# Output product: two pairs of output tiles computed together with the input features outermost, and the merge's first tile moved from GpSimd to VectorE

## The chip, the cores and the metric

One core of a Trainium2 chip runs the whole program. The metric is the device time of one execution in microseconds, from the first to the last instruction with what lies around them; the number given for a kernel is the median of its runs. The engines are named as in the profile: PE is TensorE's matrix products, PEld its weight loads, DVE is VectorE, ACT is ScalarE, POOL is GpSimd, SP issues the transfers.

## The reference

Two layers over 256 positions of 1024 features. Each layer normalises, feeds three token mixers (retention, forgetting attention, RWKV-7) from one combined projection, merges the three branches by gates, multiplies by `w_out` and adds to the residual; then comes a SwiGLU feed-forward block with its own norm. Cut to the part around the change:

```python
gates = sigmoid(gate_c).reshape(B, S, 3, D)
merged = (gates[:, :, 0] * (y_ret @ p_ret[l])
          + gates[:, :, 1] * (y_fox @ p_fox[l])
          + gates[:, :, 2] * (y_rwkv @ p_rwkv[l]))
x = x + merged @ w_out[l]
h = rmsnorm(x, ffn_norm[l])
gu = h @ w_gate_up[l]
g, u = split(gu, 2, axis=-1)
x = x + (silu(g) * u) @ w_down[l]
```

## The kernel before

Activations are held features by positions: 1024 features are eight tiles of 128 partitions by 256 positions, handled as four pairs (128 x 512). A product keeps fp32 accuracy by splitting both operands in a rounded part and the rest (`hi` and `lo`, for weights `whi` and `wlo`), and adds three matmuls for each 128 x 128 weight block: hi by whi (line L290), then the two mixed ones (L293 and L294). Function `mm3` issues them; with `late` set, the matmul that needs the activation's `lo` is the last of the three instead of the second.

Weights arrive from HBM in 1 MB transfers of 16 blocks (`raw`, three buffers) and are split in pieces of 8 blocks: ACT writes `whi` (L273, 128 x 1024) and DVE then writes `wlo` as the difference (L274). There are four buffers of each. A piece can be overwritten only when PE has done its last matmul with it.

The stage of interest is the end of the mixers. For the third branch (`bb == 2`, RWKV) a loop over the four pairs `c` computes 12 matmuls with `p_rwkv` into PSUM; DVE multiplies the result by the gate (L567, scalar_tensor_tensor, one operand in PSUM); an addition merges it in place with the sum of the other two branches (L569); and `split` turns the merged pair in `hi` (ACT, L376) and `lo` (L377). For `c == 0` the addition and the `lo` are on POOL, for the other three on DVE.

The output product follows at once in `layer`. Pair `j` of its outputs needs all eight merged tiles as inputs. For `j == 0` `gemm_halves(mx, 4)` takes 16 blocks: both output tiles over input tiles 0 to 3, then both over 4 to 7, `late`. Pairs 1 and 2 go one output tile after the other (`gemm_pair`), pair 3 by `gemm_halves` without a cut. DVE adds the residual (L491), and ACT and DVE make the norm's operands (L392, L393, L403, L406, L407).

The code is written as generators with paces. A scheduling layer turns it into a fixed list of instructions for each engine when the program is built; the priorities `hp_merge` (44) and `hp_turn` (0) act there: what stands in `early("hp_merge")`, the multiplication and the addition, is taken 44 steps earlier than its place in the code, the split is not. On the chip each engine goes through its own list.

Of the kernel before, what the change touches and what calls it, by code (L numbers as in the profile page):

```python
# [8 lines left out]
F32 = mybir.dt.float32  # L9
# [4 lines left out]
ALU = mybir.AluOpType  # L14
AX = mybir.AxisListType

P = 128
T = 256
DM = 1024
KT = DM // P  # L20
# [71 lines left out]
def pack_inputs(inp, depth=DEPTH):  # L92
    f = {k: np.asarray(v) for k, v in inp.items()}
    out = {}

    def fm(a, n):
        return a.reshape(n, P).T

    out["xt"] = np.ascontiguousarray(f["x"][0].T.reshape(KT, P, T).transpose(1, 0, 2))
    out["const"] = np.concatenate([CONSTS[k] for k in C_ORDER], 1)  # L100
    pr = []
    for l in range(depth):
        fb = np.broadcast_to(f["fox_f_bias"][l][None, :], (P, 4))
        cols = {
            "mixg": fm(f["mix_norm"][l], 8), "ffng": fm(f["ffn_norm"][l], 8), "mu": fm(f["rwkv_mu"][l], 8),
            "w0": fm(f["rwkv_w0"][l], 2), "a0": fm(f["rwkv_a0"][l], 2), "kk": fm(f["rwkv_k_k"][l], 2),
            "ka": fm(f["rwkv_k_a"][l], 2), "rk": fm(f["rwkv_r_k"][l], 2), "rgn": fm(f["rwkv_gn"][l], 2),
            "retgn": fm(f["ret_gn"][l], 2),
            "fq": np.tile(f["fox_q_norm"][l], 2)[:, None], "fk": np.tile(f["fox_k_norm"][l], 2)[:, None],
            "fb": fb, "w2a2": np.concatenate([f["rwkv_w2"][l], f["rwkv_a2"][l]], 0), "g2": f["rwkv_g2"][l],  # L110
        }
        pr.append(np.concatenate([cols[k] for k, _ in PARAMS], 1))
    out["par"] = np.ascontiguousarray(np.stack(pr))

    def tiles(w, cols, nk):
        return w[:, cols].reshape(nk, P, -1, P).transpose(1, 2, 0, 3)

    R, F, W, G = 0, 1024, 1024 + 772, 1024 + 772 + 1024
    order = np.concatenate([
        np.arange(W, W + 1024),  # L120
        np.arange(R, R + 512), np.arange(R + 768, R + 1024)])
    win, wqk, wv, wgt = [], [], [], []
    for l in range(depth):
        w = f["w_in"][l]
        t = tiles(w, order, KT)
        win.append(t.reshape(P, N_IN, 2, KT, P).transpose(1, 0, 2, 3, 4).reshape(N_IN, P, 2 * KT * P))
        wqk.append(w[:, F:F + 512].reshape(KT, P, 512).transpose(1, 0, 2).reshape(P, KT * 512))
        vf = w[:, F + 512:F + 772].reshape(KT, P, 260).transpose(1, 0, 2).reshape(P, KT * 260)
        vr = w[:, R + 512:R + 768].reshape(KT, P, 256).transpose(1, 0, 2).reshape(P, KT * 256)
        wv.append(np.concatenate([vf, vr], 1))  # L130
        wgt.append(tiles(w, np.arange(G, G + 3 * DM), KT).reshape(P, 3, 4, 2 * KT * P).transpose(1, 2, 0, 3))
    out["wqk"] = np.ascontiguousarray(np.stack(wqk))
    out["win"] = np.ascontiguousarray(np.stack(win))
    out["wgate"] = np.ascontiguousarray(np.stack(wgt))
    out["wv"] = np.ascontiguousarray(np.stack(wv))
    pp, wo, wg, wd = [], [], [], []
    for l in range(depth):
        pp.append(np.stack([tiles(f[n][l], np.arange(DM), 2).reshape(P, 2 * DM) for n in ("p_ret", "p_fox", "p_rwkv")]))
        wo.append(tiles(f["w_out"][l], np.arange(DM), KT).reshape(P, 4, 2 * KT * P).transpose(1, 0, 2))
        gu = tiles(f["w_gate_up"][l], np.arange(2 * DFF), KT).reshape(P, 2, FT // 2, 2 * KT * P)  # L140
        wg.append(gu.transpose(2, 1, 0, 3))
        wd.append(tiles(f["w_down"][l], np.arange(DM), FT).transpose(1, 0, 2, 3).reshape(4, 2, P, FT, P)
                  .transpose(0, 2, 1, 3, 4).reshape(4, P, 2 * FT * P))
    out["pp"] = np.ascontiguousarray(np.stack(pp))
    out["wo"] = np.ascontiguousarray(np.stack(wo))
    out["wg"] = np.ascontiguousarray(np.stack(wg))
    out["wd"] = np.ascontiguousarray(np.stack(wd))
    return out


class Kernel:
# [156 lines left out]
    def gemm_halves(self, xs, kcut=None, hook=None, tag="mm"):  # L308
# [19 lines left out]
                hook()  # L328
        return ps

    @staticmethod
    def run(gen):
        while True:
            try:
                next(gen)
            except StopIteration as e:
                return e.value
# [125 lines left out]
    def layer(self, l):  # L463
        tc, nc, d = self.tc, self.nc, self.d
        if l == 0:
            self.norm_start(0, "mixg")
            for j in range(4):
                self.norm_add(j, False)
                if j != 2:
                    self.piece()  # L470
        xs = self.xs
        with ExitStack() as st:
            e = st.enter_context
            self.big = e(tc.tile_pool(name="big", bufs=1))
            self.pad(self.big, 24)
            self.t2 = e(tc.tile_pool(name="t2", bufs=13))
            self.sm = e(tc.tile_pool(name="sm", bufs=1))
            self.mixers(l, xs)
            mx = self.mx

            self.norm_start(l, "ffng")
            for j in range(4):
                if j == 0:
                    ps = self.gemm_halves(mx, 4)
                elif j == 3:
                    ps = self.gemm_halves(mx)
                else:
                    ps = self.run(self.gemm_pair(mx))
                x = self.xp.tile([P, 2, T], F32, tag="x", bufs=5, name=self.nm("x"))
                for o, p in self.parts(ps):  # L490
                    nc.vector.scalar_tensor_tensor(out=x[:, o, :], in0=p, scalar=0.5, in1=self.xt[j][:, o, :], op0=ALU.mult, op1=ALU.add)  # L491
                self.xt[j] = x
                self.norm_add(j)
        self.ffn(l)
# [34 lines left out]
    def gemms(self, l, xs, rstd, rn):  # L529
        nc, d = self.nc, self.d  # L530
        fx = []
        self.need = None
        for _ in self.fox_in(l, xs, rn, fx):
            yield PACE["gemms0"]
        self.start.append(("fox", self.fox(l, fx)))
        rt = []
        for _ in self.ret_in(l, xs, rstd, rn, rt):
            yield PACE["gemms1"]
        self.start.append(("ret", self.ret(l, rt)))
        yield PACE["gemms2"]  # L540
        gates = {}
        for b in (0, 1, 2):
            for c in range(4):
                gen = self.gemm_pair(xs)
                while True:
                    try:
                        next(gen)
                    except StopIteration as e:
                        ps = e.value
                        break  # L550
                    yield PACE["gemms3"]
                g = gates[b, c] = self.big.tile([P, 2, T], F32, tag="gate", bufs=8, name=self.nm("gate"))
                nc.vector.tensor_tensor(out=g, in0=ps, in1=self.b2(rstd), op=ALU.mult)  # L553
                nc.scalar.activation(g, g, AF.Tanh, scale=0.5)
                yield PACE["gemms3"]
            if b == 0:
                continue
            for bb in ((0, 1) if b == 1 else (2,)):
                self.need = ("ret", "fox", "rwkv")[bb]
                yield PACE["gemms4"]  # L560
                self.need = None
                y = [(self.y[bb][0][:, k, :], self.y[bb][1][:, k, :]) for k in range(2)]
                for c in range(4):
                    ps = self.run(self.gemm_pair(y))
                    g, m = gates[bb, c], gates[0, c]
                    with self.early("hp_merge"):
                        nc.vector.scalar_tensor_tensor(out=g, in0=g, scalar=1.0, in1=ps, op0=ALU.add, op1=ALU.mult)  # L567
                        if bb:
                            (nc.vector if bb == 2 and c >= 1 else nc.gpsimd).tensor_tensor(out=m, in0=m, in1=g, op=ALU.add)  # L569
                    if bb == 2:  # L570
                        with self.early("hp_turn"):
                            hi, lo = self.split(self.t2, m, [P, 2, T], ("t2", "t2"), nc.gpsimd if c < 1 else nc.vector)
                        self.mx.extend((hi[:, i, :], lo[:, i, :]) for i in range(2))
                    elif c % 2:
                        yield PACE["gemms5"]
# [621 lines left out]
```

## Time and profile before

| | us |
|---|---|
| median of 3 runs | 800.09 (799.79 to 800.15) |
| the profiled execution, its own time | 800.76 |
| its span, first to last instruction | 799.0 |
| PE busy | 783.6 |
| DVE busy | 576.2 |
| ACT busy | 397.1 |
| POOL busy | 61.6 |

The span is that of one execution under the profiler; its own time lies 0.67 us above the median. Busy times of a PE matmul are modelled and overlap, so PE is read by its idle gaps and by the distance from one start to the next. The granted clock of PE is 1.00 in the whole span.

### The profile page before, as it was taken

The page shows a single profiled execution, that of the slowest core. Times are in us where ns is not written, and L with a number is a line of the kernel's source. Part 1 is how long each engine was busy: PE and PEld are TensorE (multiplying, and loading weights), DVE is VectorE, ACT ScalarE, POOL GpSimd, SP SyncE. Part 2 cuts the span into 40 slices and gives each one's busy share as a digit, 9 for nine tenths or more (in the row PEclk, how much of TensorE's full clock was granted, in tenths as well). Part 3 has the DMA queues.
Part 4 walks back from the last instruction along what each step waited for, and adds up shares of the span by engine and source line. Part 5 has one row for each costly group of instructions (what it writes and reads, how often), then busy time and mean ns, then how long its engine had stood idle before and what let it go on. Part 6 is the DMA issues. An engine that isn't in the chain of part 4 may idle for free.

```text
span 799.0 us, 16543 instructions
## 1 busy us (share of the span) xinstructions
PE 783.6 (98%) x7018; PEld 762.5 (95%) x7018; DVE 576.2 (72%) x900; ACT 397.1 (50%) x543; POOL 61.6 (8%) x83
## 2 busy tenths in 40 slices
PE   8999899999999999999999999999999999999998
PEld 6999899999999999999998988999999999999997
DVE  5897979597867666656678798877878666666453
ACT  6367445535645444445444764554456545444331
POOL 3201210031000000000023030101110000000000
PEclk9999999999999999999999999999999999999999
DMA  8565524335454554556554553452445454555650
GB/s 308 208 226 167 170 80 169 140 114 205 161 208 167 203 205 172 191 184 211 200 188 175 197 172 106 162 174 106 142 176 190 180 201 174 206 202 164 211 190 27
DMA packets 27802, 140.42 MB, mean 176 GB/s; under 512 B 7600, under 2 KB 9168, under 8 KB 12496
## 3 DMA queue, kind: packets, MB, share of 16 engines
q1 hardware_dynamic: 27728, 139.36, 50.2%
q8 instruction: 55, 0.90, 0.5%
q14 instruction: 19, 0.16, 0.1%
HBM read 136.97 MB, written 1.33 MB: 173 GB/s over the span
## 4 chain that ended last, share of the span: by engine, by line
PE 88%; DVE 6%; DMA 2%; ACT 1%; issue 1%; POOL 1%; SPq 0%; POOLq 0%; DVEq 0%; ACTq 0%
PE mm L290 26%; PE mm L294 25%; PE mm L293 25%; DVE wlo L274 2%; PE mqk L439 1%; PE mqk L438 1%; PE mqk L437 1%; ACT whi L273 1%; DMA rsw<-rqk 1%; PE pgm L762 1%; DVE rkk L745 1%; DMA raw<-in_win 1%; DMA raw<-in_pp 1%; PE mv L437 1%; PE mv L439 1%
## 5 line engine op out<-in xcount | busy, mean ns | idle before, releaser
L273 ACT CAST whi<-raw 128x1024 fp32r<-128x1024 f32 (+1 forms) x257 | 264.7, 1033 | 321.7 <-PE mm L293 232.2
L274 DVE TENSOR_TENSOR wlo<-raw,whi 128x1024 fp32r<-128x1024 f32 (+1 forms) x257 | 313.3, 1221 | 143.0 <-ACT whi L273 142.3
L290 PE MATMUL mm<-xh,whi 128*128 128x256 f32 x1312 | 368.0, 280 | 0.5 <-ACT whi L273 0.5
L294 PE MATMUL mm<-xh,wlo 128*128 128x256 f32 x1248 | 346.3, 277 | 0.7 <-DVE wlo L274 0.7
L293 PE MATMUL mm<-xl,whi 128*128 128x256 f32 x1248 | 346.3, 278 | 0.0
L290 PEld LDWEIGHTS mm<-xh,whi 128*128 128x128 f32 x1312 | 246.6, 188 | 2.8 <-issue 0.9
L294 PEld LDWEIGHTS mm<-xh,wlo 128*128 128x128 f32 x1248 | 234.4, 188 | 1.1 <-DVE wlo L274 0.9
L293 PEld LDWEIGHTS mm<-xl,whi 128*128 128x128 f32 x1248 | 234.5, 188 | 0.8 <-issue 0.5
L290 PE MATMUL mm<-hi,whi 128*128 128x256 f32 x576 | 160.1, 279 | 0.0
L294 PE MATMUL mm<-hi,wlo 128*128 128x256 f32 x544 | 150.9, 277 | 0.0
L293 PE MATMUL mm<-lo,whi 128*128 128x256 f32 x544 | 150.8, 277 | 0.0
L290 PEld LDWEIGHTS mm<-hi,whi 128*128 128x128 f32 x576 | 108.2, 188 | 0.6 <-issue 0.3
L294 PEld LDWEIGHTS mm<-hi,wlo 128*128 128x128 f32 x544 | 102.1, 188 | 0.2
L293 PEld LDWEIGHTS mm<-lo,whi 128*128 128x128 f32 x544 | 102.1, 188 | 0.1
L569 POOL TENSOR_TENSOR gate<-gate,gate 128x512 f32<-128x512 f32 x10 | 13.3, 1336 | 142.3 <-DVE gate L567 142.3
L600 DVE TENSOR_TENSOR h<-t,mm 128x512 f32<-128x512 f32 x22 | 15.1, 687 | 11.5 <-PE mm L294 8.6
L567 DVE SCALAR_TENSOR_TENSOR gate<-gate,mm 128x512 f32<-128x512 f32 x24 | 16.1, 682 | 8.6 <-PE mm L294 8.5
L597 DVE TENSOR_TENSOR t<-mm,rstd 128x512 f32<-128x512 f32 (+1 forms) x24 | 15.2, 645 | 8.5 <-PE mm L294 8.5
L553 DVE TENSOR_TENSOR gate<-mm,rstd 128x512 f32<-128x512 f32 x24 | 16.5, 689 | 3.8 <-PE mm L294 3.5
L293 PE MATMUL mm<-xh,wlo 128*128 128x256 f32 x64 | 18.0, 281 | 0.7 <-DVE wlo L274 0.7
L439 PE MATMUL mv<-whi,xl 128*128 128x260 f32 (+1 forms) x64 | 18.6, 290 | 0.0
L437 PE MATMUL mv<-whi,xh 128*128 128x260 f32 (+1 forms) x64 | 18.6, 290 | 0.0
(259 smaller groups left out, 797.9 us busy)
## 6 DMA issues: line engine op xcount, KB each, us to landing
raw<-in_wg SPq DMA_DIRECT2D x44, 1024.0 KB, 4.7
raw<-in_wgate SPq DMA_DIRECT2D x24, 1024.0 KB, 4.8
raw<-in_wd SPq DMA_DIRECT2D x16, 1024.0 KB, 5.0
raw<-in_win SPq DMA_DIRECT2D x13, 1024.0 KB, 8.0
raw<-in_wo SPq DMA_DIRECT2D x8, 1024.0 KB, 4.8
raw<-in_pp SPq DMA_DIRECT2D x6, 1024.0 KB
raw<-in_wd SPq DMA_DIRECT2D x8, 768.0 KB, 4.3
raw<-in_wqk SPq DMA_DIRECT2D x4, 1024.0 KB, 5.0
```

The source lines that it names most:

```text
L273: nc.scalar.copy(hi[:, :m * width], r)
L274: nc.vector.tensor_tensor(out=lo[:, :m * width], in0=r, in1=hi[:, :m * width].bitcast(F32), op=ALU.subtract)
L290: nc.tensor.matmul(out, wh, xh, start=first, stop=False)
L293: nc.tensor.matmul(out, wh, xl, start=False, stop=False)
L294: nc.tensor.matmul(out, wl, xh, start=False, stop=last)
L437: nc.tensor.matmul(out, xh[:, s], wh, start=first, stop=False)
L439: nc.tensor.matmul(out, xl[:, s], wh, start=False, stop=last)
L553: nc.vector.tensor_tensor(out=g, in0=ps, in1=self.b2(rstd), op=ALU.mult)
L567: nc.vector.scalar_tensor_tensor(out=g, in0=g, scalar=1.0, in1=ps, op0=ALU.add, op1=ALU.mult)
L569: (nc.vector if bb == 2 and c >= 1 else nc.gpsimd).tensor_tensor(out=m, in0=m, in1=g, op=ALU.add)
L597: nc.vector.tensor_tensor(out=t[:, o, :], in0=p, in1=self.bs(rstd, o), op=ALU.mult)
L600: nc.vector.tensor_tensor(out=h, in0=t, in1=pu, op=ALU.mult)
```

## The change

Four edits.

1. `w_out` is packed anew on the host: of the first 16 output-by-input groups, the blocks of one pair of input tiles for four output tiles now make a piece of 8, so that one piece serves pairs 0 and 1 for that pair of input tiles. The transfers keep their size and number.
2. A new `gemm_quad` computes output pairs 0 and 1 together, with the pair of input tiles (`kk`) outermost: 24 matmuls for merged pair 0, then 24 for pair 1, and so on. Each output pair accumulates in one PSUM tile. Its `mm3` isn't `late`.
3. `layer` calls it once; the two results are taken over by the residual addition one after the other, each as one 128 x 512 instruction.
4. In the merge of the third branch the addition is on POOL only for `c == 1`, and every `lo` is on DVE.

```diff
-        wo.append(tiles(f["w_out"][l], np.arange(DM), KT).reshape(P, 4, 2 * KT * P).transpose(1, 0, 2))
+        t = tiles(f["w_out"][l], np.arange(DM), KT)
+        head = t[:, :4].reshape(P, 4, 4, 2 * P).transpose(2, 0, 1, 3).reshape(2, 2, P, 8 * P).transpose(0, 2, 1, 3)
+        wo.append(np.concatenate([head.reshape(2, P, 16 * P), t[:, 4:].reshape(P, 2, 16 * P).transpose(1, 0, 2)]))
...
+    def gemm_quad(self, xs):
+
+        ps = [self.ps.tile([P, 2, T], F32, tag="mm", bufs=4, name=self.nm("mm")) for _ in range(2)]
+        for kk in range(KT // 2):
+            for j in range(2):
+                for m in range(2):
+                    for k in range(2 * kk, 2 * kk + 2):
+                        if not self.cur:
+                            self.refill()
+
+                        self.mm3(ps[j][:, m, :], self.block(), xs[k], k == m == 0, k == KT - 1 and m == 1)
+        return ps
...
                 if j == 0:
-                    ps = self.gemm_halves(mx, 4)
-                elif j == 3:
-                    ps = self.gemm_halves(mx)
-                else:
-                    ps = self.run(self.gemm_pair(mx))
+                    both = self.gemm_quad(mx)
+                ps = both[j] if j < 2 else self.run(self.gemm_pair(mx)) if j == 2 else self.gemm_halves(mx)
...
-                            (nc.vector if bb == 2 and c >= 1 else nc.gpsimd).tensor_tensor(out=m, in0=m, in1=g, op=ALU.add)
+                            (nc.vector if bb == 2 and c != 1 else nc.gpsimd).tensor_tensor(out=m, in0=m, in1=g, op=ALU.add)
                     if bb == 2:
                         with self.early("hp_turn"):
-                            hi, lo = self.split(self.t2, m, [P, 2, T], ("t2", "t2"), nc.gpsimd if c < 1 else nc.vector)
+                            hi, lo = self.split(self.t2, m, [P, 2, T], ("t2", "t2"))
```

The instruction lists differ only between the third branch's merge and the first residual additions, in both layers alike (lines of the changed kernel are 3 to 16 higher). Shown is the first layer. Names: `mm_2467`, `mm_2490`, `mm_2509` and `mm_2534` are the third branch's products for pairs 0 to 3; `gate_1200`, `gate_1319`, `gate_1443` and `gate_1505` the merged pairs 0 to 3; `hi_2486`/`lo_2487`, `hi_2505`/`lo_2506`, `hi_2530`/`lo_2531`, `hi_2549`/`lo_2550` their splits; `whi_2436`/`wlo_2437` and the next numbers are pieces of `w_out`; `mm_2554` and `mm_2555` are outputs of the output product.

DVE before, from the first multiplication of the third branch to the last split; `lo_2487` isn't in it, since POOL makes it:

```order
L567 SCALAR_TENSOR_TENSOR gate_2243<-gate_2243,mm_2467 128x512
L567 SCALAR_TENSOR_TENSOR gate_2327<-gate_2327,mm_2490 128x512
L569 TENSOR_TENSOR gate_1319<-gate_1319,gate_2327 128x512
L274 TENSOR_TENSOR wlo_2513<-raw_2510,whi_2512 128x1024
L567 SCALAR_TENSOR_TENSOR gate_2402<-gate_2402,mm_2509 128x512
L567 SCALAR_TENSOR_TENSOR gate_2464<-gate_2464,mm_2534 128x512
L569 TENSOR_TENSOR gate_1443<-gate_1443,gate_2402 128x512
L569 TENSOR_TENSOR gate_1505<-gate_1505,gate_2464 128x512
L377 TENSOR_TENSOR lo_2506<-gate_1319,hi_2505 128x512
```

DVE after, the same stretch:

```order
L580 SCALAR_TENSOR_TENSOR gate_2243<-gate_2243,mm_2467 128x512
L582 TENSOR_TENSOR gate_1200<-gate_1200,gate_2243 128x512
L580 SCALAR_TENSOR_TENSOR gate_2327<-gate_2327,mm_2490 128x512
L277 TENSOR_TENSOR wlo_2513<-raw_2510,whi_2512 128x1024
L580 SCALAR_TENSOR_TENSOR gate_2402<-gate_2402,mm_2509 128x512
L580 SCALAR_TENSOR_TENSOR gate_2464<-gate_2464,mm_2534 128x512
L582 TENSOR_TENSOR gate_1443<-gate_1443,gate_2402 128x512
L582 TENSOR_TENSOR gate_1505<-gate_1505,gate_2464 128x512
L393 TENSOR_TENSOR lo_2487<-gate_1200,hi_2486 128x512
L277 TENSOR_TENSOR wlo_2557<-raw_2510,whi_2556 128x1024
L393 TENSOR_TENSOR lo_2506<-gate_1319,hi_2505 128x512
```

The addition for pair 0 has come in behind its multiplication, that for pair 1 has left, and `lo_2487` stands ninth, behind the multiplications and additions of pairs 2 and 3, where `lo_2506` stood before; `lo_2506` is two places later, behind one more weight split.

PE before, the end of the third branch's products and the start of the output product:

```order
L294 MATMUL mm_2534<-hi_2339,wlo_2407 128x256
L290 MATMUL mm_2554<-hi_2486,whi_2436 128x256
L293 MATMUL mm_2554<-hi_2486,wlo_2437 128x256
L294 MATMUL mm_2554<-lo_2487,whi_2436 128x256
L290 MATMUL mm_2554<-hi_2486,whi_2436 128x256
```

PE after, the same place:

```order
L297 MATMUL mm_2534<-hi_2339,wlo_2407 128x256
L293 MATMUL mm_2554<-hi_2486,whi_2436 128x256
L293 MATMUL mm_2555<-hi_2486,whi_2436 128x256
L296 MATMUL mm_2554<-lo_2487,whi_2436 128x256
L297 MATMUL mm_2554<-hi_2486,wlo_2437 128x256
```

In both, two matmuls stand ahead of the first that reads `lo_2487`. Behind it, before, matmuls of pairs 0 and 1 and of a second output pair alternate; after, 22 matmuls in a row (the one shown among them) need merged pair 0 alone, and then come the 24 of pair 1.

## The prediction

> **What bounds the kernel now.** I read the page's busy times first, then the waits of PE, then the timeline of PE, DVE, POOL and ACT around the longest wait, last the busy times by stretch.
>
> ```profile
> PE 783.6 (98%) x7018; PEld 762.5 (95%) x7018; DVE 576.2 (72%) x900; ACT 397.1 (50%) x543; POOL 61.6 (8%) x83
> ```
>
> PE runs through 98% of the span. Work on another engine therefore counts only where PE waits for it, and a change that leaves the number of matmuls alone can gain at most these waits:
>
> ```profile
> PE mm L294 <- POOL lo L377: 3.1, 2, 1.6
> PE pb L748 <- DVE rkk L745: 2.9, 2, 1.5
> ```
>
> The first row is the place of this change: two waits, one in each layer, for the `lo` of merged pair 0, made by POOL. The second and all smaller ones lie outside the lists that the change touches. On PE's own rows the wait looks like this (start, duration; layer 1, then the same in layer 2):
>
> ```profile
> 197.52 0.28 PE L294 MATMUL mm<-hi,wlo 128*128 128x256 f32 x1
> 197.63 0.28 PE L290 MATMUL mm<-hi,whi 128*128 128x256 f32 x1
> 197.74 0.28 PE L293 MATMUL mm<-hi,wlo 128*128 128x256 f32 x1
> 199.57 0.39 PE L294 MATMUL mm<-lo,whi 128*128 128x256 f32 x1 [1.55 <-POOL lo L377]
> 199.80 0.28 PE L290 MATMUL mm<-hi,whi 128*128 128x256 f32 x1
> ...
> 589.98 0.28 PE L293 MATMUL mm<-hi,wlo 128*128 128x256 f32 x1
> 591.79 0.39 PE L294 MATMUL mm<-lo,whi 128*128 128x256 f32 x1 [1.53 <-POOL lo L377]
> ```
>
> Matmuls start 0.11 us apart; the third one of the output product could have started at 197.74 + 0.11 = 197.85 and starts at 199.57. That is 1.72 us lost, and 0.12 us more since the next start follows after 0.23 instead of 0.11. Layer 2: 589.98 to 591.79, 1.70 us. So the two stalls cost 1.72 + 1.70 + 0.24, about 3.7 us: all that the change could win, 0.46% of the time.
>
> Who makes PE wait? POOL and ACT in layer 1:
>
> ```profile
> 195.39 1.30 POOL L569 TENSOR_TENSOR gate<-gate,gate 128x512 f32<-128x512 f32 x1 [20.25 <-DVE gate L567]
> 197.43 2.09 POOL L377 TENSOR_TENSOR lo<-gate,hi 128x512 fp32r<-128x512 f32 x1 [0.73 <-ACT hi L376]
> ...
> 195.04 1.06 ACT L273 CAST whi<-raw 128x1024 fp32r<-128x1024 f32 x1 [1.12 <-issue]
> 196.73 1.17 ACT L376 CAST hi<-gate 128x512 fp32r<-128x512 f32 x2 [0.63 <-POOL gate L569]
> ```
>
> POOL's addition takes 1.30 us, ACT's `hi` 0.6 us, POOL's `lo` 2.09 us and ends at 199.52, 0.05 us before PE goes on. And DVE at the same time:
>
> ```profile
> 194.57 1.28 DVE L567 SCALAR_TENSOR_TENSOR gate<-gate,mm 128x512 f32<-128x512 f32 x2
> 195.88 1.36 DVE L569 TENSOR_TENSOR gate<-gate,gate 128x512 f32<-128x512 f32 x1
> 197.17 1.21 DVE L274 TENSOR_TENSOR wlo<-raw,whi 128x1024 fp32r<-128x1024 f32 x1
> 198.30 1.27 DVE L567 SCALAR_TENSOR_TENSOR gate<-gate,mm 128x512 f32<-128x512 f32 x2
> 199.50 1.28 DVE L569 TENSOR_TENSOR gate<-gate,gate 128x512 f32<-128x512 f32 x2
> 200.70 0.68 DVE L377 TENSOR_TENSOR lo<-gate,hi 128x512 fp32r<-128x512 f32 x1
> 201.30 1.21 DVE L274 TENSOR_TENSOR wlo<-raw,whi 128x1024 fp32r<-128x1024 f32 x1
> 202.44 1.28 DVE L377 TENSOR_TENSOR lo<-gate,hi 128x512 fp32r<-128x512 f32 x2
> ```
>
> DVE has no pause from 194.57 to 203.72. Its rows stand exactly in the order of its list: two multiplications, the addition for pair 1, a weight split, two multiplications, two additions, and only then the first `lo`. That `lo` (pair 1) had its input long before 200.70: ACT ended the second `hi` at 196.73 + 1.17 = 197.90. It waited 2.8 us for its turn. This row decides the case, because the change puts pair 0's `lo` in that place.
>
> **The change part by part.** *Moving the `lo`.* It is executed faster on DVE, 0.68 instead of 2.09 us, but its start is now set by the eight instructions ahead of it in DVE's list. I add them up from the rows. Successive independent instructions start closer than they last: 0.60 us for a 128 x 512 one (199.50 + 1.20 = 200.70 for two) and 1.13 to 1.14 for a weight split (197.17 to 198.30). An addition that needs the multiplication just ahead starts 0.03 after its end (194.57 + 1.28 = 195.85, then 195.88).
>
> - 194.57: multiplication for pair 0, ends 195.25. Nothing ahead of it in any list has changed, so this start stands.
> - 195.28: addition for pair 0. POOL is idle then, so I take 0.68 (half the row of the two at 199.50, by 1.28 - 0.60), not the 1.36 of the row at 195.88; ends 195.96.
> - 195.88: multiplication for pair 1, ends 196.56.
> - 196.48: weight split `wlo_2513`; its `whi` is ready at 195.04 + 1.06 = 196.10. The next can start at 197.62.
> - 197.62 and 198.22: multiplications for pairs 2 and 3. PE's last product for pair 3 starts at 197.52 and lasts 0.28, so it isn't late.
> - 198.82 and 199.42: additions for pairs 2 and 3. 200.02: `lo` of pair 0, ends 200.70.
>
> *The addition for pair 1 on POOL.* It meets `wlo_2513` on DVE. What such a meeting costs can be read elsewhere in the trace:
>
> ```profile
> 162.32 2.77 POOL L569 TENSOR_TENSOR gate<-gate,gate 128x512 f32<-128x512 f32 x2 [45.52 <-DVE gate L567]
> 163.92 2.25 DVE L274 TENSOR_TENSOR wlo<-raw,whi 128x1024 fp32r<-128x1024 f32 x1 [0.32 <-ACT whi L273]
> ```
>
> POOL was running first, until 165.09, and DVE's split took 2.25 instead of 1.23: it hardly moved until POOL was done. In the rows quoted above the split at 197.17 came first, kept its 1.21, and POOL's `lo` of 197.43 ended 1.14 after it. The first one holds the other up. The multiplications at 198.30, which read PSUM, ran beside POOL undisturbed. In the changed kernel POOL can begin 0.14 after the multiplication for pair 1 (before: 195.25 to 195.39), at 196.70. DVE's split started at 196.48, so POOL waits until about 197.71 and needs 1.14 to 1.30 more, to 198.85 to 199.01. The addition for pair 2, due at 198.82, is a kind of instruction that POOL holds up: 0.03 to 0.19 late, I take 0.13. The `lo` of pair 0 then ends at 200.83, and PE goes on 0.05 later at 200.88.
>
> Against 199.57 that is 1.31 us later in layer 1. Layer 2 has the same lists and starts its first multiplication at 586.80:
>
> ```profile
> 586.80 1.27 DVE L567 SCALAR_TENSOR_TENSOR gate<-gate,mm 128x512 f32<-128x512 f32 x2
> ```
>
> So 586.80 + 6.31 = 593.11 against 591.79, 1.32 later. Sum: +2.63 us.
>
> *The new order of the output product.* The count of matmuls is the same, 96 for the two output pairs. Its use would be to cover a late pair 1: 22 matmuls that need only pair 0 stand ahead. After 200.88 these last 0.23 + 21 x 0.117, to about 203.5. In DVE's list the `lo` of pair 1 follows that of pair 0 by 0.60 + 1.14, starts at 201.9 and ends at 202.6: ready 0.9 us early. Pair 2's follows at once and is needed 24 matmuls later. But the cover lies behind the wait for pair 0, and only two matmuls stand ahead of that wait, as before. I cost the order itself at nothing. Its unknown is PE's pace:
>
> ```profile
> 199.57:206.86 7.29, 7.29 (x62) 7.29 (x62) 5.01 (x9) 2.74 (x5) 0.11 (x1) 1.00 0.39 144
> 206.86:214.15 7.29, 7.29 (x67) 7.29 (x66) 7.17 (x11) 6.04 (x9) 0.00 (x0) 1.00 0.47 156
> ```
>
> In the 7.29 us behind the stall PE starts 62 matmuls (first column of counts), in the next 7.29 it starts 67, at the same granted clock of 1.00. Starts are 0.117 apart instead of 0.113. If that belongs to the old mixture of outputs, it goes, and 62 x 0.0044 = 0.27 us in each layer comes back; if it follows the stall, it stays or lasts longer by as much. I take no change, and ±0.5 us for both layers.
>
> *Late residual additions.* Output pair 0 is now finished about when pair 1 is, so DVE gets two additions and two norm operands at once. What must not be late is the sum of squares at the start of the feed-forward block:
>
> ```profile
> 224.91 0.42 DVE L415 TENSOR_TENSOR tot<-acc 128x256 f32<-128x256 f32 x1
> 226.92 0.50 PE L419 MATMUL pn<-con,tot 128*128 128x1 f32 x4
> ```
>
> It is ready at 225.33 and used at 226.92, 1.6 us of room, and two output pairs of 48 matmuls, 10.9 us, lie between the quad and the block for DVE to catch up. Cost nothing. The packing on the host moves no bytes on the chip: the 1 MB transfers stay.
>
> *Sum.* 800.76 + 2.63 = 803.39 for the profiled execution. That one is 0.67 above the median of the runs, 800.09, so the median should become 802.72, say 802.7, 0.33% slower.
>
> **Rivals.** *POOL first* (10%). If POOL's addition for pair 1 wins against `wlo_2513`, the split is held up as in the row at 163.92, by 2.25 - 1.23 = 1.02 us, and everything behind it on DVE with it: 2.63 + 2.04 = 4.67, so 804.8. For it: the 1.36 of the addition at 195.88, twice its length beside POOL. Against it: DVE has 0.22 us of lead. PE would then stand still about 3.9 us, against 2.9 in my forecast. [...]
>
> *The `lo` leaves early* (6%), the case on the other side. If DVE made the `lo` of pair 0 as soon as its `hi` is there (ACT is free at 196.10, `hi` lasts 0.6, to 196.7) and the split of weights is through at 197.62, it would end at 198.30 and PE go on at 198.35: 1.22 us earlier in each layer, 797.65. It decides where the `lo` starts ahead of the additions for pairs 2 and 3, before 198.82. For it: 0.68 against 2.09 us for the same instruction. Against it: the `lo` at 200.70, which had its input 2.8 us before and kept its place. [...]
>
> *Most of it given back* (8%). The slow pace disappears with the new order (-0.54) and the addition for pair 2 isn't held up (-0.26): 2.63 - 0.80 = 1.83, 801.9. For it: the slow stretch begins at the stall's place in both layers. Against it: nothing shows what sets the pace.
>
> **How the numbers follow.** My forecast has 76% and by itself the range 801.9 to 803.8: the upper end is reached if the addition for pair 0 loses on DVE the 0.68 us that the row at 195.88 lost (200.70 + 0.68 = 201.38, PE at 201.43, 1.86 in each layer, 3.7 in both). With 0.2 us for the spread of a median, 801.7 to 803.9 leaves out the two rivals with 10% and 6%. About 0.2% (1.6 us) is what a measurement of this kernel can tell from no change: 801.7 is that bound. Faster 6% (the early `lo`), within it 5% (the larger part of the give-back case), slower 89%.
>
> **What would show it.** In the changed profile PE waits twice for DVE's `lo` (now L393), about 2.8 us each, where it waited twice for POOL; POOL's `lo` is gone. The list of DVE shows the `lo` of pair 0 some 5.6 us behind the first multiplication, and POOL's addition for pair 1 about 2.3 us long beside an undisturbed weight split of 1.2. PE has no second wait at pair 1, and its waits outside the stage are as before. [...]

## The result, and the profile after

| | before | after |
|---|---|---|
| median of the runs shown with the result | 800.09 (799.12 to 800.97, 5 runs) | 804.55 (803.75 to 806.98, 5 runs) |
| the profiled execution | 800.76 | 806.98 |
| its span | 799.0 | 805.2 |

The ratio is 1.0063, with a 95% interval of 1.0050 to 1.0076. The change makes the kernel 4.5 us slower. The forecast was 802.7, with 801.7 to 803.9: the sign is right, the time lies outside the range.

The page's busy times hardly move; POOL has two instructions fewer, and PE's busy time grows by 3.5 us although it issues the same matmuls:

```profile
PE 787.1 (98%) x7018; PEld 765.8 (95%) x7018; DVE 576.4 (72%) x900; ACT 397.5 (49%) x543; POOL 59.0 (7%) x81
```

The same work that keeps PE busy for longer is a first hint at its speed. Next, PE's waits (total, times, longest):

```profile
PE mm L296 <- DVE lo L393: 5.5, 2, 2.7
PE pb L761 <- DVE rkk L758: 2.9, 2, 1.5
```

POOL's `lo` is gone, and PE waits twice for DVE's, 2.7 us each. DVE's timeline in layer 1 (start, duration), and POOL's only instruction there:

```profile
195.37 0.69 DVE L582 TENSOR_TENSOR gate<-gate,gate 128x512 f32<-128x512 f32 x1
...
196.57 1.22 DVE L277 TENSOR_TENSOR wlo<-raw,whi 128x1024 fp32r<-128x1024 f32 x1
197.71 1.28 DVE L580 SCALAR_TENSOR_TENSOR gate<-gate,mm 128x512 f32<-128x512 f32 x2
198.90 1.29 DVE L582 TENSOR_TENSOR gate<-gate,gate 128x512 f32<-128x512 f32 x2
200.10 0.69 DVE L393 TENSOR_TENSOR lo<-gate,hi 128x512 fp32r<-128x512 f32 x1
...
196.81 2.12 POOL L582 TENSOR_TENSOR gate<-gate,gate 128x512 f32<-128x512 f32 x1 [21.57 <-DVE gate L580]
```

The `lo` of pair 0 starts at 200.10 behind two multiplications and two additions, as forecast (200.02, held up to 200.15). Up to here nothing is missing. PE's rows behind the wait show what is:

```profile
200.85 0.39 PE L296 MATMUL mm<-lo,whi 128*128 128x256 f32 x1 [2.74 <-DVE lo L393]
...
201.31 0.28 PE L296 MATMUL mm<-lo,whi 128*128 128x256 f32 x1
201.42 0.31 PE L297 MATMUL mm<-hi,wlo 128*128 128x256 f32 x1
201.54 0.41 PE L293 MATMUL mm<-hi,whi 128*128 128x256 f32 x1
201.75 0.41 PE L296 MATMUL mm<-lo,whi 128*128 128x256 f32 x1
201.96 0.41 PE L297 MATMUL mm<-hi,wlo 128*128 128x256 f32 x1
```

PE goes on at 200.85 (forecast 200.88), starts a matmul every 0.12 us, and from 201.54 on every 0.21 us, each of them 0.41 long instead of 0.28. The busy times by stretch (PE and its count first; the granted clock is the third number from the end) put a name to it:

```profile
201.54:205.00 3.46, 3.46 (x19) 3.46 (x18) 2.19 (x4) 0.00 (x0) 0.11 (x1) 0.51 0.57 168
205.00:208.14 3.14, 3.14 (x29) 3.14 (x29) 1.23 (x1) 1.15 (x2) 0.00 (x0) 1.00 0.35 149
596.56:603.80 7.24, 7.24 (x48) 7.24 (x49) 4.12 (x5) 1.10 (x2) 0.11 (x1) 0.76 0.41 145
```

For 3.4 us the granted clock is 0.51, then 1.00 again. The count of 19 matmuls stands for a stretch that holds 32 at the full clock (last experiment below). Layer 2 has the same (0.76 over 7.24 us). In steps of 2 us, no other part of the span in which PE works has a granted clock below 0.97.

To measure a stage free of what happens elsewhere I use the distance between two rows of PE: `pv<-con,ysq`, ahead of the merge, and `pn<-con,tot`, ahead of the feed-forward block. Before (first row; its `pn` at 226.92 stands in the prediction) it is 46.06 us, after (the other two) 48.94:

```profile
180.86 0.49 PE L953 MATMUL pv<-con,ysq 128*128 128x128 f32 x3
...
180.94 0.49 PE L966 MATMUL pv<-con,ysq 128*128 128x128 f32 x3
229.88 0.39 PE L435 MATMUL pn<-con,tot 128*128 128x1 f32 x3
```

Below it is "the stage". Layer 2 goes from 46.04 to 48.71. So 2.88 + 2.67 = 5.55 us of the 6.22 between the two profiled executions lie in the stage, and 0.67 outside it.

### The profile page after: what moved, and what is told of

Read it like the earlier page. It is cut to its first block, busy times and chain, and to the rows that moved or that the text cites. A ratio compares the mean times of both kernels' runs of the same rounds, so it can differ in the third digit from the quotient of the medians.

```text
span 805.2 us, 16542 instructions
## 1 busy us (share of the span) xinstructions
PE 787.1 (98%) x7018; PEld 765.8 (95%) x7018; DVE 576.4 (72%) x900; ACT 397.5 (49%) x543; POOL 59.0 (7%) x81
## 4 chain that ended last, share of the span: by engine, by line
PE 86%; DVE 8%; DMA 3%; ACT 1%; issue 1%; SPq 1%; POOL 0%; DVEq 0%; POOLq 0%; ACTq 0%
PE mm L293 25%; PE mm L297 25%; PE mm L296 25%; DVE wlo L277 2%; PE mqk L455 1%; PE mqk L454 1%; PE mqk L453 1%; DMA rsw<-rqk 1%; ACT whi L276 1%; DVE rkk L758 1%; PE pgm L775 1%; DMA raw<-in_pp 1%; DMA raw<-in_win 1%; DVE gate L580 1%; PE mv L453 1%
## 5 line engine op out<-in xcount | busy, mean ns | idle before, releaser
L296 PE MATMUL mm<-lo,whi 128*128 128x256 f32 x576 | 161.4, 280 | 5.5 <-DVE lo L393 5.5
L297 PE MATMUL mm<-hi,wlo 128*128 128x256 f32 x576 | 161.4, 280 | 0.0
L296 PEld LDWEIGHTS mm<-lo,whi 128*128 128x128 f32 x576 | 109.8, 191 | 6.0 <-DVE lo L393 5.9
L297 PEld LDWEIGHTS mm<-hi,wlo 128*128 128x128 f32 x576 | 109.7, 190 | 0.2
```

Of the source, the lines that this page charges most:

```text
L296: nc.tensor.matmul(out, wh, xl, start=False, stop=False)
L297: nc.tensor.matmul(out, wl, xh, start=False, stop=last)
```

## The experiments

The theory after the result: DVE's list makes PE resume 1.2 us later in each layer, as forecast, and the idle stretch before it drops PE's clock to a half for 3.4 us, which was not. Rivals: the quad order itself costs time, or POOL's addition does. The first four kernels were compared with 23 runs of before (median 800.08).

**The `lo` of pair 0 moved forward.** The changed kernel, with only this split raised in the list:

```diff
-                        with self.early("hp_turn"):
+                        with (self.tc.high_priority(44) if c == 0 else nullcontext()):
```

> The changed kernel with one thing altered: the lo of merged pair 0 gets the priority of the merge, so that in DVE's list it stands ahead of the multiplications and additions for pairs 2 and 3 (directly behind one weight split). List-order theory: PE goes on at about 198.45 instead of 200.85 in layer 1 (stall about 0.6 us instead of 3.0), the granted clock stays 1.00, and pair 1 may cost 0.2 us a layer: 797.9 to 798.4. If POOL's addition for pair 1 gets in ahead of this lo and holds it up, PE goes on at about 199.65: 800.2. Rival, the new order of the output product itself is what costs: 802 or more.

801.41 us (11 runs), ratio 1.0011, interval 1.0002 to 1.0020. DVE, POOL and PE in layer 1:

```profile
196.91 1.22 DVE L277 TENSOR_TENSOR wlo<-raw,whi 128x1024 fp32r<-128x1024 f32 x1
198.04 1.76 DVE L393 TENSOR_TENSOR lo<-gate,hi 128x512 fp32r<-128x512 f32 x1
...
197.14 2.11 POOL L582 TENSOR_TENSOR gate<-gate,gate 128x512 f32<-128x512 f32 x1 [21.57 <-DVE gate L580]
...
199.85 0.39 PE L296 MATMUL mm<-lo,whi 128*128 128x256 f32 x1 [1.41 <-DVE lo L393]
```

The `lo` starts at 198.04, right behind the weight split, but takes 1.76 us instead of 0.69: POOL's addition, held up by the split, ends at 199.25, and the `lo` has 0.55 us left after that. The stage is 46.05 and 45.94 us, as before. With the better place the loss in the stage is gone; POOL's addition takes away what the place would win beyond that. The median is 1.2 us above the 800.2 expected for this case, and the stage doesn't hold that rest.

**The quad order alone** (edits 1 to 3, the engines as before):

```diff
-(nc.vector if bb == 2 and c != 1 else nc.gpsimd).tensor_tensor(out=m, in0=m, in1=g, op=ALU.add)
+(nc.vector if bb == 2 and c >= 1 else nc.gpsimd).tensor_tensor(out=m, in0=m, in1=g, op=ALU.add)
...
-hi, lo = self.split(self.t2, m, [P, 2, T], ("t2", "t2"))
+hi, lo = self.split(self.t2, m, [P, 2, T], ("t2", "t2"), nc.gpsimd if c < 1 else nc.vector)
```

> Edits 1 to 3 alone: the quad order and the new packing, with the merge's engines as before (POOL adds and splits pair 0). List-order theory: PE waits for POOL's lo until 199.57 as before, the quad order is worth nothing here, the clock stays 1.00: 800.1 within 0.6. Rival, the quad order costs: 802.5 to 804.5.

800.77 us (11 runs), ratio 1.0011, interval 1.0002 to 1.0019. The waits are nearly those of before (1.66 us on average, 1.54 before); the stage is 45.93 and 45.91, 0.13 us shorter in each layer:

```profile
PE mm L296 <- POOL lo L393: 3.3, 2, 1.7
```

The order by itself doesn't make the kernel slow.

**The engines alone** (the kernel before with edit 4, the reverse of the diff above):

> Edit 4 alone: POOL adds pair 1 only and DVE makes every lo, with the output product in the order of before. List-order theory: DVE's list puts the lo of pair 0 behind the merges of pairs 2 and 3, PE goes on at about 200.88, 2.6 us lost in both layers, and since five matmuls instead of two stand ahead of the wait the idle time is about 2.5 us; with what the half clock takes after it (nothing to 3.1 us) 802.7 to 805.8. Rival, the quad order costs: 800.1.

803.20 us (6 runs), ratio 1.0040, interval 1.0028 to 1.0052. PE resumes at 200.84 as after the whole change, with a shorter wait, since five matmuls stand ahead of it and not two:

```profile
PE mm L294 <- DVE lo L377: 4.0, 2, 2.0
```

In the profiled execution the clock is 1.00 and the stage 46.70 and 46.73, +0.64 and +0.69. Its time is 802.08. The other five runs have a mean granted clock of 0.996 to 0.998, and four of them are slower, 802.65 to 804.62.

**PE kept busy in the wait.** The changed kernel with 22 extra matmuls of pair 0's `hi`, into a PSUM tile that nobody reads, ahead of the wait:

```diff
+                        if k == m == j == 0:
+                            pf = self.ps.tile([P, T], F32, tag="fr", bufs=2, name=self.nm("fill"))
+                            for i in range(22):
+                                self.nc.tensor.matmul(pf, blk[0], xs[k][0], start=i == 0, stop=i == 22 - 1)
```

> The changed kernel with 22 extra matmuls on data that is there (hi of pair 0 by the first whi, into a PSUM tile that nothing reads) ahead of the wait for lo, about 2.5 us of PE work in the middle of the stall. Theory that the half clock comes from PE's idle time: the stall's end stays at about 200.85, no half clock, 802.7. Rival, the half clock belongs to the new order of matmuls or to something else: 804.5 as the changed kernel, or later.

803.06 us (5 runs, 802.39 to 804.08), ratio 1.0039, interval 1.0027 to 1.0051. The wait's end does not move (19.90 us behind `pv`, as after the change; 18.71 before), PE is idle only 0.24 us ahead of it, and the clock stays whole in both layers:

```profile
PE mm L296 <- DVE lo L398: 0.5, 2, 0.2
...
200.34:207.58 7.24, 7.24 (x64) 7.24 (x65) 4.79 (x6) 2.10 (x2) 0.11 (x1) 1.00 0.41 145
```

The stage is 47.01 and 47.00 us. More work on PE makes the kernel 1.5 us faster than the changed one. So the lost time has two parts: the list (this run against before) and the clock (the changed kernel against this run). Of this run's 3.0 us over before, 1.9 lie in the stage.

The next four were compared with 19 runs of before (median 799.74).

**POOL out of the stage, and the splits raised.** The addition of pair 1 goes to DVE too:

```diff
-(nc.vector if bb == 2 and c != 1 else nc.gpsimd).tensor_tensor(out=m, in0=m, in1=g, op=ALU.add)
+(nc.vector if bb == 2 else nc.gpsimd).tensor_tensor(out=m, in0=m, in1=g, op=ALU.add)
...
-                        with self.early("hp_turn"):
+                        with self.tc.high_priority(44):
```

> The changed kernel with the addition of pair 1 on VectorE as well and the splits of the merge raised by 44 places, so that GpSimd has no work in this stage and VectorE's list reads: multiplication, addition of pair 0, multiplication of pair 1, the split of a weight tile, lo of pair 0, addition of pair 1, and so on. If what spoiled the run with lo moved ahead was GpSimd's waiting addition slipping in ahead of it (lo took 1.76 us there instead of 0.68 and matmul resumed at 199.85), then lo here runs undisturbed right behind the weight split: it starts near 197.7 on the profile's clock of the kernel before, takes 0.68, and TensorE resumes near 198.4, with a wait of about 0.6 us per layer instead of 1.7. That is 1.1 us per layer ahead of before: 797.8 us, and 797.0 to 798.7 with the pace of the quad order. Rival: the place in the list is not what decides, or the added addition on VectorE delays the next pairs (lo of pairs 1 to 3, 0.6 us later each, become waits of TensorE): then 799.5 us or more, with a new wait for lo of pair 1.

798.02 us (797.16 to 798.75, 7 runs), ratio 0.9977, interval 0.9967 to 0.9988: faster than before and than the changed kernel. DVE and PE in layer 1:

```profile
196.40 1.22 DVE L277 TENSOR_TENSOR wlo<-raw,whi 128x1024 fp32r<-128x1024 f32 x1
197.53 0.69 DVE L393 TENSOR_TENSOR lo<-gate,hi 128x512 fp32r<-128x512 f32 x1
198.13 0.68 DVE L582 TENSOR_TENSOR gate<-gate,gate 128x512 f32<-128x512 f32 x1
...
198.27 0.38 PE L296 MATMUL mm<-lo,whi 128*128 128x256 f32 x1 [0.34 <-DVE lo L393]
```

At nearly the same place as in the first experiment the `lo` takes 0.69 us and not 1.76. The stage is 44.62 us in both layers, 1.44 and 1.42 less than before. The addition of pair 1 on DVE makes nobody wait.

**The same engines and places with the old order of the output product:**

> The kernel before with the same engines and the same raise of 44 places as the run above, but with the output product in its old order. If the quad order is worth nothing (as the run with the quad order alone said, ratio 1.0011), this gives the same time as the run above: 797.8 us, 797.0 to 798.7, with matmul resuming near 198.4. If the quad order matters once the stall is short (four interleaved tiles need lo of pair 1 later or earlier than the halves order does), the two runs differ by 0.5 us or more, and a wait for lo of pair 1 stands in one of them and not in the other.

800.06 us (11 runs), ratio 1.0004, interval 0.9995 to 1.0013. The rival won: without the quad order the gain is gone. PE resumes as early as in the run above (17.50 us behind `pv` against 17.51), but the stage is 45.61 and 45.51. The new wait is not for pair 1, as the text above had it, but for pair 2, which PE reaches before DVE does. DVE (its last row holds the `lo` of pair 2), then PE:

```profile
201.15 1.29 DVE L569 TENSOR_TENSOR gate<-gate,gate 128x512 f32<-128x512 f32 x2
202.36 1.22 DVE L274 TENSOR_TENSOR wlo<-raw,whi 128x1024 fp32r<-128x1024 f32 x1
203.49 0.69 DVE L377 TENSOR_TENSOR lo<-gate,hi 128x512 fp32r<-128x512 f32 x1
...
204.23 0.38 PE L294 MATMUL mm<-lo,whi 128*128 128x256 f32 x1 [0.49 <-DVE lo L377]
```

The old order asks for pair 2 after 24 matmuls of pairs 0 and 1, the quad after 48. The start at 204.23 follows one at 203.47, so it could have come at 203.58: 0.65 us, and 0.12 more behind it. That is 0.77 of the 0.9 to 1.0 us between the two orders in each layer; the rest I didn't separate.

**A later `lo`.** The addition of pair 1 on DVE, nothing raised, so that one more instruction stands ahead of the `lo`:

> The changed kernel with the addition of pair 1 on VectorE as well and nothing raised: one more addition (0.60 us) stands ahead of lo of pair 0 in VectorE's list, and nothing of GpSimd beside it. By the list alone lo starts near 200.6 and TensorE resumes near 201.35, a wait of 3.2 us against 2.74: 0.5 us per layer later than in the changed kernel. Theory of the idle clock: a wait of 3.2 us is followed by 3.41 us at half clock in both layers in every run, at 1.55 us each, so 800.1 + 2 x (1.8 + 1.55) = 806.8 us, 805.5 to 807.5, with a granted clock of 0.996. Rival, that the extra of the changed kernel over its list has nothing to do with the wait: 804.55 + 1.0 = 805.5 us or less, with clock 1.00.

807.64 us (806.60 to 808.75, 4 runs), ratio 1.0097, interval 1.0084 to 1.0110. The wait grows by 0.60 us, and half clock follows it in both layers:

```profile
201.87 0.38 PE L296 MATMUL mm<-lo,whi 128*128 128x256 f32 x1 [3.34 <-DVE lo L393]
...
202.80:206.26 3.46, 3.46 (x19) 3.46 (x18) 1.96 (x4) 0.21 (x1) 0.11 (x1) 0.51 0.56 194
```

The stage is 49.54 and 49.32, 0.60 and 0.61 over the changed kernel. The median lies 0.14 us above the expected range.

**A slightly shorter wait.** Three extra matmuls instead of 22:

> The changed kernel with three extra 128x256 matmuls of hi by the weights' hi half into a tile of PSUM that nobody reads, ahead of the wait for lo of pair 0: they shorten TensorE's idle stretch from 2.74 to about 2.4 us and leave the end of the wait where it is. With 2.0 us of wait the clock stayed at 1.00 (engines alone), with 2.74 it fell in both layers. If the limit lies above 2.4 us, no half clock appears and the time is that of the run with 22 extra matmuls, 802.8 to 803.1 us; if it lies below, the half clock stays and the time is that of the changed kernel, 804 to 805 us. The theory does not say which; the other explanation, that the half clock belongs to the interleaved order and not to the idle stretch, gives 804.5 us whatever the idle length.

804.98 us (802.98 to 806.55, 6 runs), ratio 1.0064, interval 1.0050 to 1.0078. The wait is 2.40 us and half clock still follows in both layers, so what limit there is lies lower than 2.4 us. With the run of 22 extra matmuls, the same order without half clock, this leaves the idle stretch as the cause and not the interleaved order. In layer 2 it begins with the first matmul, where after the change it began 0.9 us behind it:

```profile
594.88 0.58 PE L296 MATMUL mm<-lo,whi 128*128 128x256 f32 x1 [2.39 <-DVE lo L398]
595.26 0.41 PE L297 MATMUL mm<-hi,wlo 128*128 128x256 f32 x1
```

**Both kernels once more**, on another chip, each unchanged, against 15 runs of before (median 800.18).

> The kernel before, unchanged, as one more kernel beside its own runs. In the profiles so far every variant lost 0.5 to 1 us against before outside the merge's stage, most of it in the wait for dn ahead of pn in the second layer (0.20 us in the profile of before, 0.5 to 1.2 in the others). If that is the scatter of a DMA round trip, this run shows a dn wait between 0.2 and 1.2 us too and a ratio of 1.000 within 0.001; if the wait belongs to the variants, it is 0.2 again here. The stretch from pv of the merge to pn of the next norm should be 46.05 us in both layers again (it was 46.06 and 46.04), with the wait for lo at 18.7 us after pv.

Before: 800.31 us, ratio 0.9998, interval 0.9989 to 1.0007. PE resumes 18.71 us behind `pv` again, the wait for `dn` is 0.4 us where it was 0.2, and the stage is 46.06 in layer 1 but 45.80 in layer 2, 0.25 under the expected. So a few tenths of one profile say nothing of a variant.

> The changed kernel, unchanged, once more on another chip. The theory: the wait for lo of pair 0 ends 19.9 us after pv as in every kernel with this list (18.7 before), and TensorE's half clock comes behind it in one or both layers, 3.41 us long, so the stretch from pv to pn is 48.7 to 48.9 us in a layer with the half clock and 47.0 in one without (as in the run with 22 extra matmuls). The time is 803 to 807 us, by how many of the two layers are hit: about 803 with none, 804.6 with one, 806.2 with both. Rival, that the first runs' half clock was an accident of that chip: 802.7 us, clock 1.00.

After: 804.49 us (803.31 to 805.53, 5 runs), ratio 1.0054, interval 1.0040 to 1.0068. The profiled execution is the lucky one of the five. It has the same wait, and no half clock in either layer:

```profile
201.37 0.38 PE L296 MATMUL mm<-lo,whi 128*128 128x256 f32 x1 [2.74 <-DVE lo L393]
...
202.06:205.52 3.46, 3.46 (x32) 3.46 (x31) 2.44 (x5) 1.05 (x1) 0.11 (x1) 1.00 0.52 163
```

Its time is 803.31 and its stage 47.18 and 47.19. The same kernel with half clock in both layers, in the first profile, had 48.94 and 48.71: one half-clock stretch costs 1.5 to 1.8 us. Whether it comes differs from one execution to the next. The mean granted clock of each timed run shows how often (one such stretch takes 3.4/2/800 = 0.002 off it):

| kernel | PE's wait for `lo`, us | runs | mean granted clock | runs at 0.998 or less |
|---|---|---|---|---|
| 22 extra matmuls | 0.24 | 5 | 0.9996 | 0 |
| all on DVE, `lo` raised | 0.34 | 7 | 0.9997 | 1 |
| all on DVE, old order | 0.22, then 0.49 | 11 | 0.9987 | 5 |
| `lo` of pair 0 raised | 1.41 | 11 | 0.9990 | 4 |
| before | 1.55 | 68 | 0.9994 | 12 |
| quad order alone | 1.66 | 11 | 0.9992 | 2 |
| engines alone | 2.02 | 6 | 0.9975 | 5 |
| 3 extra matmuls | 2.40 | 6 | 0.9963 | 6 |
| the change (both jobs) | 2.74 | 10 | 0.9972 | 9 |
| all on DVE, `lo` late | 3.34 | 4 | 0.9950 | 4 |

Up to 1.7 us of wait a run has such a stretch now and then, more often (5 of 11) with the old order and all on DVE. The one that the profile of the quad order alone caught lies at the program's start (a granted clock of 0.76 from 11 to 18 us), not in the stage; in the profile of all on DVE in the old order (mean 0.997) the matmuls around the wait for pair 2 in layer 1 keep their 0.28 us. From 2.0 us on nearly every run has one or two, and with 3.3 us each has about two or more. In the stage itself a profile shows them at 2.40 us and above; at 2.02 us only the mean clocks speak for them.

## Why the prediction was wrong, and where it was right

- **The place of the `lo`: right.** Forecast to start at 200.02 plus a hold-up of 0.13, measured 200.10; PE at 200.88, measured 200.85. DVE's first multiplication there started 0.08 us later than before (194.65 against 194.57), so the list alone gives 200.10: the hold-up by POOL did not occur, and the close agreement is in part luck. Behind `pv` the resume moves from 18.71 to 19.90 us, +1.19, where the forecast had 1.31; the missing hold-up is the difference. POOL's addition took 2.12 us beside an undisturbed split of 1.22, as forecast (2.3 and 1.2).
- **The term for the list: +2.63, a little large.** With the clock whole the change costs 2.27 us in the two stages (47.18 + 47.19 against 46.06 + 46.04), and the execution 803.31. The run with PE kept busy has a median of 803.06. Both lie in the forecast's own range of 801.9 to 803.8.
- **The step that failed: nothing for the clock behind the stall.** I set the clock's share in the sum to zero for a stall of 2.9 us by my count. That was my estimate; no row of the trace stood for it. The nearest rows, waits of 1.55 us at a clock of 1.00, excluded nothing at 2.7. The missing term is the number of half-clock stretches in the two stages, between none and two, times 1.5 to 1.8 us. From the mean clocks of the runs of the change and of before (0.9972 and 0.9994) it is 0.0022 / 0.0021, about 1.0 stretch more than before, an estimate of 1.5 to 1.8 us; with the 2.27 of the list that is 803.9 to 804.2, and the median was 804.55. The other 0.4 to 0.7 us lie outside the stage or in the scatter, and no run separates them; the wait for `dn`, 0.9 us after the change against 0.2 and 0.4 before, may be a part. Waits of 2.40 and 2.74 us were enough to bring the half clock.
- **The half clock as the runs show it.** It lasts 3.4 us, begins anywhere from 0.3 us ahead of the resume to 1.5 us behind it (layers 2 and 1 with three extra matmuls), and comes in one execution and not in another: 2.40 us of wait brought it in both layers of a profile, 2.74 us in both layers of one and in neither of the other.
- **The quad order at nothing: right alone, wrong in company.** Alone it changes the stage by -0.13 us per layer. Where the `lo` comes late, it adds 0.48 and 0.46 (46.70 and 46.73 with the engines alone, 47.18 and 47.19 with both), where two matmuls and not five stand ahead of the wait; three matmuls at 0.113 us are 0.34 of that, and the rest wasn't separated. Where the `lo` comes early it is worth 2.0 us (798.02 against 800.06). I had priced it at one state of the lists only.
- **The rivals.** "POOL first" didn't happen: the split kept its 1.22 us, and that its 804.8 lies near the measured 804.55 is chance. "The `lo` leaves early" was the other side, at 797.65; made real by a raised split, a POOL without work and the quad order it gave 798.02. Its condition was incomplete: with POOL's addition waiting, the place alone gave 801.41. Of "Most of it given back" one part came: the addition for pair 2 wasn't held up (-0.24). The slow pace stayed with the new order: in the repeated run of the change, with the clock whole, PE starts 62 matmuls in the 7.29 us behind the stall, as before. In all 0.36 us of the 2.63 were given back.

## What to carry to other kernels

Moving an instruction to a faster engine (here 0.69 us on DVE for 2.09 on POOL) puts it into another list; what counts is what stands ahead of it there, so read its place before its duration, and raise it if its consumer is the bound. Count a stall of the matrix engine twice: once by its length, once by the clock that it may lose behind it. Here that second part began at waits somewhere between 1.7 and 2.4 us and was nearly as large as the first. The same wait of 2.74 us brought it in one execution and not in another, so give it as a chance times a price. And price two edits together as well as apart: here neither half of the change won anything alone, not even the engines with the `lo` early and POOL out of the way (800.06); only both halves together with these did (798.02).

## What the hardware showed unexpectedly

- The half clock has the same length in both layers of the changed kernel, 3.41 us, and no fixed distance to the wait. It begins 0.69 us behind the resume at 200.85 in layer 1 and 0.92 us behind that at 596.56 in layer 2:

```profile
201.54:204.95 3.41, 3.41 (x19) 3.41 (x18) 2.19 (x4) 0.00 (x0) 0.11 (x1) 0.50 0.57 168
597.48:600.89 3.41, 3.41 (x18) 3.41 (x17) 1.97 (x4) 0.13 (x1) 0.11 (x1) 0.50 0.62 202
```

The granted clock also falls to 0.50 behind PE's last work, in the changed kernel at 805.70, about 4.5 us after its last matmul. The length of the wait alone doesn't decide: in the two profiled executions of the change, two of the four waits of 2.74 us had no half clock behind them, while both waits of 2.40 us with three extra matmuls had it. What decides was not shown; no run was made to test it.
- POOL's addition, waiting for DVE, got in between two DVE instructions that otherwise follow each other without a pause. In the run with the `lo` of pair 0 raised it was held up by the split (2.11 us, against 1.30 for pair 0's addition in the kernel before), and then held up the `lo` behind the split (1.76 us instead of 0.69). In the changed kernel the same addition (196.81, 2.12 us) met two multiplications from PSUM at that place, which took their 1.28 us, and ended at 198.93.
